# An encoder block on one core: one ring of raw weight tiles through the last gate/up block and the first down group, and its forms reloaded later and closer together

## The chip, the core and the metric

The kernel runs on one core of one Trainium2 chip. The metric is the device time of a whole execution in microseconds (us), taken as the median of three runs. TensorE (PE), VectorE (DVE), ScalarE (ACT), GpSimd (POOL) and SyncE (SP) each work through a queue of their own in order; SP, ACT and POOL also issue DMAs.

## What is computed

One encoder layer in fp32 on 512 tokens of width 2048: a norm, an input projection, two attention mixers, an output projection, and then the part in which the change lies, SwiGLU with D_FF = 5632, and a last norm.

```python
h2 = rmsnorm(x, g_ffn[layer])
gate, up = jnp.split(jnp.einsum('bsd,df->bsf', h2, w_gate_up[layer]), 2, axis=-1)
x = x + jnp.einsum('bsf,fd->bsd', jax.nn.silu(gate) * up, w_down[layer])
return rmsnorm(x, g_final)
```

## The kernel before

Every fp32 product is made of split numbers: a high half rounded to fp32r and a low half, the rest, and three matmuls (high by high, high by low, low by high; lines 227 to 229). The SwiGLU products are done in blocks of columns by a scheme with seven forms, m1 to m7: each form is a product of sums of quarter matrices, which saves one product in eight and needs sums of weights.

**Blocks and units.** Gate and up take eleven blocks, f0 = 0, 4, ..., 40 (block 40 is the last). A block runs the chain m1, m7, m6, m2, m5, m4, m3 with eight units each, 56 units; a unit is six matmuls. Down takes three groups of 6, 8 and 8 pairs (`DOWN_PAIRS`), two column blocks a group: the two blocks of six pairs (d6) have 42 units, the four of eight pairs (d8) 56.

**Weights.** Two units share one split of 128x1024 weights. It is made from raw tiles of 512 KB, loaded on SP's queue (line 272; 28 a gate/up block, 12 a d6 block), some combined first on VectorE (line 972). ScalarE makes the high half (line 836), VectorE the low half (line 839), into a ring of four `wide` pairs. All raws of one tag form a ring: a load is written into the program, a few units ahead of its use (up to 20 us by the kernel's own count), as soon as fewer than `RAWS[tag]` tiles are alive. Blocks 0 to 36 use twelve (`craw`), whose tiles are handed on by a list (`kept_raws`, for the tags in `KEPT_TAGS`); the last block has a ring of ten of its own (`craw40`), the d6 blocks another ten (`draw6`), the d8 blocks fifteen (`draw8`).

**Results of gate/up.** Snapshots of forms (`s1`, `s7`, `s6`) and their sums turn into silu(gate) * up. This is transposed by DMA (SP, line 1257), put together on ScalarE (line 1263), the sums of quarter matrices for the down product are made on VectorE (line 378), and all seven forms of a pair go to DRAM from the tile `pair` by a POOL DMA (`store`, line 1266). Two such stores belong to a block; in the last block the second comes 55 units after the last unit of m3, in the second d6 block.

**Forms of a down group.** They are read back, form by form, into the `arena` where the old forms have been used (`next_forms`). Of a group of six pairs a form comes in two parts, four pairs (512 KB) and two pairs (256 KB), into two `fr` tiles in turn: load on ScalarE's DMA queue (line 1306), high half on ScalarE (line 1309), low half on VectorE (line 1312). `turn` is the unit of the high half; the load is hooked five units ahead of it and the low half two units behind, and turns lie at least four units apart. The turns of the first group, counted from the first unit of the last gate/up block, are m1 8 and 12, m7 20 and 24, m6 32 and 36, m2 44 and 48, m5 56 and 60, m4 68 and 72, m3 80 and 84. The last block's snapshots are `slot` tiles; a down block's evictions (`ev`, line 1333) go to six more, which POOL adds to DRAM (`x1d`, line 1334).

All is written out by hand: at each unit the loop issues loads and splits that are due, the unit's matmuls, and the hooked steps; each engine's queue keeps that order.

Of the kernel before, what the change touches and what calls it, by code (L numbers as in the profile page):

```python
# [11 lines left out]
F32 = mybir.dt.float32  # L12
# [8 lines left out]
P = 128  # L21
# [4 lines left out]
KD = D // P  # L26
# [23 lines left out]
SPILLED = {"A": 4, "B": 6}  # L50
TWINS = 8
WIDE = 4
WIDE_AHEAD = 9.5
RAWS = {"raw": 6, "craw": 12, "craw1": 24, "craw0": 24, "kraw": 9, "craw40": 10, "draw6": 10, "draw8": 15}
KEPT_TAGS = ("craw",)
W_TILES = {"wi": 10, "wo": 12}
DOWN_PAIRS = (6, 8, 8)
ORDER = ("m1", "m7", "m6", "m2", "m4", "m5", "m3")
# [1 line left out]
EVICT = 6  # L60
# [15 lines left out]
def encoder_block(ctx, tc, x, w_in, g_q_a, g_k_a, w_out, w_gate_up, w_down, g_final, x_t, gains, c_ident, c_mask,  # L76
# [15 lines left out]
    def slot(base, dtype=F32, shape=(P, 512)):  # L92
        return sp.tile(list(shape), dtype, tag="s", name=nm(base))
# [25 lines left out]
    stage = wp.tile([P, 20, 512], F32, tag="stage", bufs=1, name="stage")  # L119
    homes = deque(stage[:, n] for n in range(8, 20))  # L120
    homing = [True]
    kept_raws = deque()
    extra_homes, retired = {}, []

    def more_homes(name, tile):
# [189 lines left out]
    def hook(n, f):  # L315
        hooks.setdefault(n, []).append(f)
# [886 lines left out]
    def hold(name, shape, dtype=F32):  # L1203
        if name not in held:
            held[name] = sp.tile([P] + list(shape), dtype, tag=name, bufs=1, name=nm(name))
        return held[name]

    forms_dram = dp.tile([P, 7, NFF // 2, 256], F32, tag="forms", name="forms")
    def gate_up_block(f0):
# [1 line left out]
        st = {}  # L1211

        def tile2(name):
            st[name] = [slot(name) if f0 == 40 else hold(f"{name}{t}", [512]) for t in range(2)]
            return st[name]

        def snap(form, name):
# [60 lines left out]
        for n, late in enumerate((3, 4, 6, 7)):  # L1278
            box.after("m3", late, lambda n=n: planes(("glo", "uhi")[n // 2], n // 2, n % 2))
            box.after("m3", late + 7, lambda n=n: turn(n))  # L1280
        for j, late in enumerate((23, 50 if f0 == 40 else 36)):
            for n, part in enumerate(((1, 0, 4, 1024), (0, 2, 4, 0), (0, 0, 2, 256))):
                box.after("m3", late + n, lambda j=j, part=part: merge(j, *part))
            box.after("m3", late + 3, lambda: pair_sums(hpart[0]))
            box.after("m3", late + 5, lambda j=j: store(f0 // 2 + j))
        return box

    for f in range(0, NFF, 4):
        box = gate_up_block(f)

    def load_x1(c, rows):
        for t in rows:
# [3 lines left out]
    def next_forms(box, first, pairs):  # L1296
        seq, turns = sorted(CHAIN, key=box.at.get), [0]

        def ready(form, h):
            m, st = ORDER.index(form), {}  # L1300
            lo_q, n = 4 * h, min(4, pairs - 4 * h)
            hi, lo = (form_tile(m, slice(lo_q, lo_q + n))[:, :, j] for j in range(2))

            def load():
                st["t"] = in_turn(frs, 2, [P, 4, 256], F32, "fr")[:, :n]
                nc.scalar.dma_start(st["t"], forms_dram[:, m, first + lo_q:first + lo_q + n])

            def split_hi():
                nc.scalar.activation(hi, st["t"], AF.Copy)

            def split_lo():
                nc.vector.tensor_tensor(lo, st["t"], f32(hi), op=OP.subtract)
            turn = max(box.at[form] + 4 * seq.index(form) + 4 * h + 1, turns[-1] + 4)
            turns.append(turn)
            hook(turn - 5, load)
            hook(turn, split_hi)
            hook(turn + 2, split_lo)
        for form in seq:
            for h in range(-(-pairs // 4)):
                ready(form, h)  # L1320
# [3 lines left out]
    def down_block(first, pairs, cb, last):  # L1324
# [3 lines left out]
        def add(form, i, j):  # L1328
            def go():
                for t in range(2):  # L1330
                    row = 2 * i + t
                    e = in_turn(evs, EVICT, [P, 512], F32, "ev")
                    nc.scalar.activation(e, box.bank_of(form)[t], AF.Copy, scale=r2["r"][:, row:row + 1])  # L1333
                    nc.gpsimd.dma_start(x1_dram[2 * cb + j, row], e, accum_op=OP.add)  # L1334
                if form in LAST_OF_BANK:
                    box.done(form)
            box.after(form, 0, go)
# [129 lines left out]
    def load_raws(n):  # L1467
        while done["load"] < len(units) and at[done["load"]] <= at[n] + units[done["load"]].load_ahead:
            for raw in units[done["load"]].raws:
                if raw.t is None:  # L1470
                    for r in live:
                        if last_use[r] < done["lo"] and r.homed and homing[0] and not any(r.t is h for h in retired):
                            homes.append(r.t)
                        elif last_use[r] < done["lo"] and not homing[0] and r.tag in KEPT_TAGS:
                            kept_raws.append(r.t)
                    live[:] = [r for r in live if last_use[r] >= done["lo"]]
                    if homing[0] and len(homes) <= (2 if xs[KD - 1] is None else 4 if done["load"] < 24 else 0):
                        return
                    if homing[0] and raw.tag == "raw" and sum(r.tag == "raw" for r in live) >= 2:
                        return  # L1480
                    if sum((r.tag == "raw") == (raw.tag == "raw") for r in live) >= RAWS[raw.tag]:
                        return
                    live.append(raw)
                    raw.load()
            done["load"] += 1
# [115 lines left out]
```

## Time and profile before

| | us |
|---|---|
| runs | 1962.06, 1963.46, 1964.12 |
| median | 1963.46 |
| the profiled execution | 1962.45 |
| its span in the profile | 1960.7 |
| TensorE busy | 1940.9 (99%) |
| VectorE busy | 1537.2 (78%) |
| ScalarE busy | 1129.3 (58%) |
| last gate/up block starts | 1444.2 |
| first and second d6 block start | 1526.2, 1583.4 |
| first d8 block starts | 1647.2 |

Busy times are those of the span. The profile is one execution; 1.75 us lie around its span. Line numbers are those of the kernel before. `PEclk` in the windows is the granted clock of TensorE, 1.00 for 2.4 GHz and 0.50 for 1.2 GHz; the DMA share is that of the core's sixteen DMA engines.

### The profile page before, as it was taken

The page shows a single profiled execution, that of the slowest core. Times are in us where ns is not written, and L with a number is a line of the kernel's source. Part 1 is how long each engine was busy: PE and PEld are TensorE (multiplying, and loading weights), DVE is VectorE, ACT ScalarE, POOL GpSimd, SP SyncE. Part 2 cuts the span into 40 slices and gives each one's busy share as a digit, 9 for nine tenths or more (in the row PEclk, how much of TensorE's full clock was granted, in tenths as well). Part 3 has the DMA queues.
Part 4 walks back from the last instruction along what each step waited for, and adds up shares of the span by engine and source line. Part 5 has one row for each costly group of instructions (what it writes and reads, how often), then busy time and mean ns, then how long its engine had stood idle before and what let it go on. Part 6 is the DMA issues. An engine that isn't in the chain of part 4 may idle for free.

```text
span 1960.7 us, 24582 instructions
## 1 busy us (share of the span) xinstructions
PE 1940.9 (99%) x8727; PEld 1600.7 (82%) x8727; DVE 1537.2 (78%) x2012; ACT 1129.3 (58%) x1649; POOL 140.2 (7%) x184
## 2 busy tenths in 40 slices
PE   9999999999999999999999999999999999999998
PEld 7888888888888888888888888888887887888886
DVE  7987778887775697778778778778787877787886
ACT  7655554565455565555555555555555656555555
POOL 1000011000000000000000000000000121111121
PEclk9999999999999999999999999999999999999999
DMA  9777693144342466858758757767678789868865
GB/s 345 236 258 236 210 280 108 59 145 156 102 151 97 172 209 188 295 150 274 262 151 284 242 173 278 224 197 283 200 231 288 202 220 296 225 157 252 225 146 167
DMA packets 256252, 410.35 MB, mean 209 GB/s; under 512 B 62912, under 2 KB 90048, under 8 KB 256000
## 3 DMA queue, kind: packets, MB, share of 16 engines
q1 hardware_dynamic: 225296, 322.17, 50.5%
q0 software_dynamic: 22480, 60.57, 12.4%
q10 hardware_dynamic: 8352, 26.05, 4.0%
q8 instruction: 68, 1.11, 0.2%
q14 instruction: 56, 0.46, 0.1%
HBM read 334.52 MB, written 62.65 MB: 203 GB/s over the span
## 4 chain that ended last, share of the span: by engine, by line
PE 91%; DVE 4%; issue 2%; DMA 2%; ACT 1%; POOL 0%; SPq 0%; DVEq 0%; POOLq 0%; ACTq 0%
PE b L229 29%; PE b L228 29%; PE b L227 29%; PE b L612 1%; DMA raw<-in_w_gate_up_dram 1%; DVE wide L839 1%; POOL x1d L1334 0%; PE b L1170 0%; DVE raw L972 0%; PE b L562 0%; DMA forms<-pair 0%; DMA raw<-in_w_in_dram 0%; DVE x L1124 0%; DMA raw<-in_w_down_dram 0%; DVE w L305 0%
## 5 line engine op out<-in xcount | busy, mean ns | idle before, releaser
L836 ACT ACTIVATE wide<-raw 128x1024 fp32r<-128x1024 f32 x462 | 487.2, 1059 | 474.3 <-PE b L229 265.7
L228 PE MATMUL b<-wide,arena 128*128 128x512 f32 x1848 | 721.4, 390 | 4.4 <-DVE wide L839 4.4
L227 PE MATMUL b<-wide,arena 128*128 128x512 f32 x1848 | 721.2, 390 | 3.1 <-ACT wide L836 2.5
L839 DVE TENSOR_TENSOR wide<-raw,wide 128x1024 fp32r<-128x1024 f32 x462 | 562.5, 1223 | 205.2 <-ACT wide L836 195.7
L229 PE MATMUL b<-wide,arena 128*128 128x512 f32 x1848 | 721.0, 390 | 0.0
L228 PEld LDWEIGHTS b<-wide,arena 128*128 128x128 f32 x1848 | 347.9, 188 | 77.8 <-DVE wide L839 5.6
L227 PEld LDWEIGHTS b<-wide,arena 128*128 128x128 f32 x1848 | 348.0, 188 | 76.0 <-ACT wide L836 2.9
L229 PEld LDWEIGHTS b<-wide,arena 128*128 128x128 f32 x1848 | 348.0, 188 | 72.6
L972 DVE TENSOR_TENSOR raw<-raw,raw 128x1024 f32<-128x1024 f32 x264 | 321.5, 1220 | 11.9 <-DMA raw<-in_w_gate_up_dram 11.8
L228 PE MATMUL b<-tw,arena 128*128 128x512 f32 x396 | 154.3, 390 | 0.6 <-DVE tw L895 0.6
L229 PE MATMUL b<-tw,arena 128*128 128x512 f32 x396 | 154.2, 389 | 0.0
L227 PE MATMUL b<-tw,arena 128*128 128x512 f32 x396 | 154.1, 389 | 0.0
L892 ACT ACTIVATE tw<-stage 128x512 fp32r<-128x512 f32 x140 | 85.5, 628 | 69.4 <-DVE stage L972 45.0
L895 DVE TENSOR_TENSOR tw<-stage,tw 128x512 fp32r<-128x512 f32 x140 | 93.9, 688 | 22.0 <-ACT tw L892 21.2
L218 ACT ACTIVATE pTh<-b 128x512 fp32r<-128x512 f32 x64 | 38.2, 597 | 101.0 <-PE b L612 95.7
L227 PE MATMUL b<-w,arena 128*128 128x512 f32 x240 | 95.8, 399 | 0.0
L229 PE MATMUL b<-w,arena 128*128 128x512 f32 x240 | 93.9, 391 | 0.0
L228 PE MATMUL b<-w,arena 128*128 128x512 f32 x240 | 93.5, 390 | 0.0
L1334 POOL DMA_DIRECT2D x1d<-ev x76 | 66.0, 962 | 318.0 <-ACT ev L1333 295.3
L378 DVE TENSOR_TENSOR pair<-pair 128x256 f32<-128x256 f32 x120 | 46.6, 422 | 53.6 <-ACT pair L1263 29.4
L228 PEld LDWEIGHTS b<-tw,arena 128*128 128x128 f32 x396 | 74.3, 188 | 16.8 <-DVE tw L895 1.5
L229 PEld LDWEIGHTS b<-tw,arena 128*128 128x128 f32 x396 | 74.3, 188 | 15.8 <-DVE arena L346 0.4
(229 smaller groups left out, 2107.0 us busy)
## 6 DMA issues: line engine op xcount, KB each, us to landing
raw<-in_w_gate_up_dram SPq DMA_DIRECT2D x308, 512.0 KB, 6.1
raw<-in_w_down_dram SPq DMA_DIRECT2D x88, 512.0 KB, 6.9
stage<-in_w_in_dram SPq DMA_DIRECT2D x111, 256.0 KB, 5.3
forms<-pair POOLq DMA_DIRECT2D x22, 896.0 KB, 8.2
x1d<-ev POOLq DMA_DIRECT2D x76, 256.0 KB, 6.2
fr<-forms ACTq DMA_DIRECT2D x35, 512.0 KB, 6.2
raw<-in_w_out_dram SPq DMA_DIRECT2D x32, 512.0 KB, 4.2
stage<-in_w_in_dram SPq DMA_DIRECT2D x90, 128.0 KB, 3.4
```

Source lines behind the costliest of these rows:

```text
L218: nc.scalar.activation(hi, src, AF.Copy)
L227: nc.tensor.matmul(dst, ah, bh, start=start, stop=False, skip_group_check=chained)
L228: nc.tensor.matmul(dst, ah, bl, start=False, stop=False, skip_group_check=chained)
L229: nc.tensor.matmul(dst, al, bh, start=False, stop=stop, skip_group_check=chained)
L378: nc.vector.tensor_tensor(out, x, y, op=op)
L612: nc.tensor.transpose(ps[:, t * P:(t + 1) * P], self.p[t][:, kb * P:(kb + 1) * P], ident)
L836: nc.scalar.activation(self.hi, self.src, AF.Copy)
L839: nc.vector.tensor_tensor(self.lo, self.src, f32(self.hi), op=OP.subtract)
L892: nc.scalar.activation(self.pair[:, 0], self.src, AF.Copy)
L895: nc.vector.tensor_tensor(self.pair[:, 1], self.src, f32(self.pair[:, 0]), op=OP.subtract)
L972: nc.vector.tensor_tensor(t[dst], t[src[0]], t[src[1]], op=OP.add if form == "m6" else OP.subtract)
L1334: nc.gpsimd.dma_start(x1_dram[2 * cb + j, row], e, accum_op=OP.add)
```

## The change

- One ring of twelve raws goes on from block 36 through the last block and the d6 blocks: `craw40` and `draw6` are among the tags whose tiles are handed on. At unit 28 of the last block two of the twelve tiles leave the list (`DROP_AT`), and ten remain. `draw8` becomes 16.
- The last block's snapshots use the held tiles `s1`, `s6`, `s7`, as other blocks do, and the evictions of the down blocks use these six tiles in turn.
- The second store of the last block and what leads to it come ten units earlier (40 instead of 50 units after m3).
- The first group's forms are reloaded from unit 7 + 30 of the last block on in steps of three. The turns become m1 37 and 40, m7 43 and 46, m6 49 and 52, m2 55 and 58, m5 61 and 64, m4 67 and 70, m3 73 and 76. For all groups turns may lie three units apart; the load is four units ahead of the turn and the low half one behind.

```diff
+RELOAD_AT = 30
+RELOAD_STEP = 3
+DROP_AT = 28
-RAWS = {"raw": 6, "craw": 12, "craw1": 24, "craw0": 24, "kraw": 9, "craw40": 10, "draw6": 10, "draw8": 15}
-KEPT_TAGS = ("craw",)
+RAWS = {"raw": 6, "craw": 12, "craw1": 24, "craw0": 24, "kraw": 9, "craw40": 10, "draw6": 10, "draw8": 16}
+KEPT_TAGS = ("craw", "craw40", "draw6")
...
-            st[name] = [slot(name) if f0 == 40 else hold(f"{name}{t}", [512]) for t in range(2)]
+            st[name] = [hold(name, [2, 512])[:, t] for t in range(2)]
...
-        for j, late in enumerate((23, 50 if f0 == 40 else 36)):
+        for j, late in enumerate((23, 40 if f0 == 40 else 36)):
...
+    last_gate = box.at["m1"] - KD // 2 + 1
...
-            turn = max(box.at[form] + 4 * seq.index(form) + 4 * h + 1, turns[-1] + 4)
+            turn = max(box.at[form] + 4 * seq.index(form) + 4 * h + 1, turns[-1] + RELOAD_STEP)
+            if first == 0:
+                turn = max(box.at[form] + 1, box.at["m1"] + RELOAD_AT, turns[-1] + RELOAD_STEP)
             turns.append(turn)
-            hook(turn - 5, load)
+            hook(turn - RELOAD_STEP - 1, load)
             hook(turn, split_hi)
-            hook(turn + 2, split_lo)
+            hook(turn + RELOAD_STEP - 2, split_lo)
...
-                    e = in_turn(evs, EVICT, [P, 512], F32, "ev")
+                    if not evs:
+                        evs.extend(held[name][:, t] for name in ("s1", "s6", "s7") for t in range(2))
+                    evs.append(evs.pop(0))
+                    e = evs[-1]
...
                         elif last_use[r] < done["lo"] and not homing[0] and r.tag in KEPT_TAGS:
-                            kept_raws.append(r.t)
+                            if n >= last_gate + DROP_AT and dropped[0] < RAWS["craw"] - RAWS["draw6"]:
+                                dropped[0] += 1
+                            else:
+                                kept_raws.append(r.t)
...
-                    if sum((r.tag == "raw") == (raw.tag == "raw") for r in live) >= RAWS[raw.tag]:
+                    most = RAWS["craw"] if raw.tag == "craw40" and n < last_gate + DROP_AT else RAWS[raw.tag]
+                    if sum((r.tag == "raw") == (raw.tag == "raw") for r in live) >= most:
```

Three places in the queues show what this moves. On ScalarE, before, behind the silu of the last block's `s1` (`wide` are the splits, `fr` the tiles of the reloads, `pair` and `turned` the putting together of the results):

```order
L836 ACTIVATE wide_525_5840<-raw_556_10700 128x1024
L1263 ACTIVATE pair_467_5381<-turned_550_6452 128x1024
L1236 ACTIVATE s1_565_10828<-s1_565_10828,fixed_81 128x512
L1236 ACTIVATE s1_566_10829<-s1_566_10829,fixed_81 128x512
L836 ACTIVATE wide_527_5842<-raw_558_10720 128x1024
L1263 ACTIVATE pair_467_5381<-turned_550_6452 128x512
L1309 ACTIVATE arena5_85<-fr_562_10790 128x2x256
L1263 ACTIVATE pair_467_5381<-turned_550_6452 128x512
L836 ACTIVATE wide_529_5844<-raw_560_10738 128x1024
L1306 DMA fr_561_10789<-forms_138 128x1024
L836 ACTIVATE wide_531_5846<-raw_564_10820 128x1024
```

The same place in the changed program:

```order
L1266 ACTIVATE pair_467_5381<-turned_547_6449 128x1024
L1239 ACTIVATE s1_544_6071<-s1_544_6071,fixed_81 128x512 x2
L839 ACTIVATE wide_527_5842<-raw_521_5811 128x1024
L1266 ACTIVATE pair_467_5381<-turned_547_6449 128x512
L1311 DMA fr_549_11034<-forms_138 128x512
L1266 ACTIVATE pair_467_5381<-turned_547_6449 128x512
L1314 ACTIVATE arena2_84<-fr_548_11033 128x4x256
L839 ACTIVATE wide_529_5844<-raw_524_5838 128x1024
L1311 DMA fr_548_11033<-forms_138 128x1024
L839 ACTIVATE wide_531_5846<-raw_535_5906 128x1024
L1314 ACTIVATE arena2_84<-fr_549_11034 128x2x256
```

Before, one reload's high half and one load stand among four splits; now two loads and two high halves stand among three, and the reload in work is that of m1 where it was that of m6.

On POOL, the last of the stores of forms among the adding writes of the evictions, before:

```order
L1334 DMA x1d11_127<-ev_598_11376 128x512
L1334 DMA x1d20_130<-ev_599_11377 128x512
L1334 DMA x1d21_131<-ev_600_11378 128x512
L1334 DMA x1d32_136<-ev_601_11379 128x512
L1334 DMA x1d33_137<-ev_602_11380 128x512
L1266 DMA forms_138<-pair_467_5381 896x1x256
L1334 DMA x1d22_132<-ev_597_11375 128x512
```

And now:

```order
L1344 DMA x1d11_127<-s1_544_6071 128x512
L1269 DMA forms_138<-pair_467_5381 896x1x256
L1344 DMA x1d20_130<-s6_546_6203 128x512
L1344 DMA x1d21_131<-s6_546_6203 128x512
L1344 DMA x1d32_136<-s7_545_6137 128x512
L1344 DMA x1d33_137<-s7_545_6137 128x512
L1344 DMA x1d22_132<-s1_544_6071 128x512
```

The store is four adding writes further ahead.

On SP, the loads of the end of the second d6 block and the beginning of the first d8 block (`raw_615` and `raw_616` are the last two loads of the second d6 block, the waits named DMASW are on POOL's stores of forms), before:

```order
L272 DMA raw_614_11725<-in_w_down_dram 128x2x512 [waits DMAHW0_49,DVE_49]
L272 DMA raw_615_11848<-in_w_down_dram 128x2x512 [waits DMASW4_49,DMASW5_49,DMASW3_49,DMASW6_49,DMASW2_49,DMASW7_49,DMASW1_49,DMAHW1_49,DMASW0_49,DMAHW5_49,DVE_49,Activation_49]
L272 DMA raw_616_11870<-in_w_down_dram 128x2x512 [waits DMAHW6_49]
L272 DMA raw_617_11946<-in_w_down_dram 128x2x512 [waits DMAHW7_49]
L272 DMA raw_618_11964<-in_w_down_dram 128x2x512 [waits DMAHW0_49]
```

And now, where `raw_538` and `raw_535` are the last two of the d6 block and `raw_550` is the first of the d8 block:

```order
L275 DMA raw_538_5940<-in_w_down_dram 128x2x512 [waits DMAHW4_49,DVE_49]
L275 DMA raw_535_5906<-in_w_down_dram 128x2x512 [waits DMAHW6_49,DVE_49,Activation_49]
L275 DMA raw_550_11880<-in_w_down_dram 128x2x512 [waits DMASW5_49,DMASW4_49,DMASW6_49,DMASW3_49,DMASW7_49,DMASW2_49,DMAHW7_49,DMASW1_49,DMASW0_49]
L275 DMA raw_551_11897<-in_w_down_dram 128x2x512 [waits DMAHW0_49]
L275 DMA raw_552_11908<-in_w_down_dram 128x2x512 [waits DMAHW1_49]
```

The wait for the stores has moved from the eleventh load of the second d6 block to the first load of the d8 block.

## Rows read from the trace of the kernel before

**Rows 1.** The chain that ended last, by engine (section 4 of the page)
```profile
PE 91%; DVE 4%; issue 2%; DMA 2%; ACT 1%; POOL 0%; SPq 0%; DVEq 0%; POOLq 0%; ACTq 0%
```

**Rows 2.** Waits of TensorE, 1368 to 1960: waited for, us in total, times, longest
```profile
PE b L228 <- DVE wide L839: 4.4, 3, 3.5
PE b L227 <- ACT wide L836: 2.5, 1, 2.5
```

**Rows 3.** Windows, block by block: blocks 36 and 40, both d6, first d8
```profile
core 0: us, PE busy (x) PEld busy (x) DVE busy (x) ACT busy (x) POOL busy (x), PEclk, DMA share, GB/s
1368.10:1444.20 76.10, 76.10 (x337) 63.04 (x336) 60.12 (x63) 43.02 (x48) 1.82 (x2) 1.00 0.68 218
1444.20:1526.20 82.00, 78.36 (x337) 64.06 (x336) 67.99 (x72) 48.97 (x56) 1.81 (x2) 0.98 0.82 260
1526.20:1583.40 57.20, 57.20 (x254) 47.27 (x253) 47.15 (x47) 39.66 (x47) 7.96 (x9) 1.00 0.80 212
1583.40:1647.20 63.80, 60.58 (x254) 49.33 (x253) 45.95 (x44) 38.83 (x46) 16.45 (x19) 0.95 0.92 247
1647.20:1723.30 76.10, 76.10 (x337) 63.05 (x336) 61.60 (x54) 44.89 (x50) 12.13 (x14) 1.00 0.87 235
```

**Rows 4.** Chain pieces before the first stop: start us, us, what
```profile
1482.61 6.55 DMA raw<-in_w_gate_up_dram
1489.18 1.24 DVE raw L972
```

**Rows 5.** Timeline around it: start us, us, instruction, idle before and releaser
```profile
1490.32 1.22 DVE L839 TENSOR_TENSOR wide<-raw,wide 128x1024 fp32r<-128x1024 f32 x1
1491.59 0.50 PE L228 MATMUL b<-wide,arena 128*128 128x512 f32 x1 [3.46 <-DVE wide L839]
```

**Rows 6.** Chain pieces around the second stop
```profile
1609.32 5.97 DMA forms<-pair
1615.54 4.61 DMA raw<-in_w_down_dram
1620.23 1.06 ACT wide L836
1621.32 1.24 DVE wide L839
1622.60 0.79 PE b L228
1623.39 0.43 PE b L229
...
1629.42 0.23 PE b L229
```

**Rows 7.** Waits of the SP queue, 1444 to 1660
```profile
SPq L272 <- DMA forms<-pair: 37.5, 1, 37.5
```

**Rows 8.** Windows: the busiest stretch, and the stretches behind the two stops
```profile
1494.60:1526.20 31.60, 31.42 (x136) 25.68 (x135) 29.96 (x34) 20.14 (x23) 0.91 (x1) 0.98 1.01 366
...
1492.30:1495.70 3.40, 3.40 (x10) 2.63 (x9) 3.37 (x4) 1.35 (x2) 0.00 (x0) 0.50 0.99 357
1622.00:1628.80 6.80, 6.20 (x15) 4.85 (x16) 5.20 (x6) 5.39 (x7) 1.72 (x2) 0.50 1.06 357
```

**Rows 9.** VectorE's low halves of reloads, and the window, 1494.6 to 1547
```profile
L1312 DVE TENSOR_TENSOR arena<-fr,arena 128x1024 fp32r<-128x1024 f32 x4 | 4.9, 1222 | 0.0
...
L1312 DVE TENSOR_TENSOR arena<-fr,arena 128x512 fp32r<-128x512 f32 x3 | 2.1, 687 | 0.0
1494.60:1547.00 52.40, 52.22 (x228) 42.92 (x227) 50.36 (x54) 37.02 (x42) 4.47 (x5) 0.99 0.89 275
```

**Rows 10.** ScalarE's high halves of the large reloads, 1494.6 to 1547
```profile
L1309 ACT ACTIVATE arena<-fr 128x1024 fp32r<-128x1024 f32 x4 | 4.2, 1050 | 1.0 <-DMA fr<-forms 1.0
```

**Rows 11.** Issues 1494 to 1583; landings of fr 1526 to 1600, then 1440 to 1600
```profile
fr<-forms ACTq DMA_DIRECT2D x4, 512.0 KB, 8.1
DMA to landing us min/median/max: 3.9/6.6/8.5
DMA to landing us min/median/max: 2.7/6.3/8.5
```

**Rows 12.** Timeline of VectorE and of TensorE at the next block's start
```profile
1519.64 1.23 DVE L839 TENSOR_TENSOR wide<-raw,wide 128x1024 fp32r<-128x1024 f32 x1
1526.21 0.39 PE L227 MATMUL b<-wide,arena 128*128 128x512 f32 x1
```

More of the change, by code (lines that the diff above doesn't have):

```diff
@@ L121, in encoder_block @@
     homing = [True]
-    kept_raws = deque()
+    kept_raws, dropped = deque(), [0]
     extra_homes, retired = {}, []
```

## The prediction

> **What bounds the kernel now.** I read four views in this order: the shares of the chain, the waits of TensorE, its blocks one by one, and the two places where it stops. The chain that ended last is 91% TensorE [rows 1], and from block 36 to the last down block TensorE waits only for splits of weights: 4.4 us in three waits on VectorE's low half and 2.5 us in one wait on ScalarE's high half [rows 2]. So nothing but those stops, and what they do to the clock, can be won in the region of the change. Block by block [rows 3]: block 36, 56 units, takes 76.1 us with PE busy for all of it (1.36 us a unit); the last gate/up block takes 82.0 us for the same 336 matmuls, 5.9 more; the first down block (42 units) takes 57.2, the second 63.8, 6.6 more. The first block of eight pairs is back at 76.1. The two excesses, 12.5 us, are all that there is to take.
>
> Stop A: in the last gate block a raw leaves SP's queue at 1482.61, lands 6.55 us later, and the combination that needs it starts at 1489.18 [rows 4]. TensorE has by then stood for 3.46 us, to 1491.59 [rows 5]. Stop B: the first load of the second down block's tail is released by the landing of the last forms store (issued 1609.32, 5.97 us), lands 4.61 us after its own issue, and goes through both splits to the matmul at 1622.60 [rows 6]; SP stood for 37.5 us on that one store [rows 7]. After both stops the granted clock is 0.50, the 1.2 GHz level, for 3.4 and 6.8 us [rows 8], and the matmuls there follow at 0.43 us instead of 0.23 [rows 6]: eight and sixteen of them, some 1.6 and 3.2 us of the 5.9 and 6.6.
>
> **The ring.** The last gate block keeps twelve raws, as block 36 has, until its unit 28, and inherits them from the ring instead of starting ten of its own. Block 36 with twelve has no stop at all [rows 3], and the stop at unit 32 (43.5 us, or 32 units, into the block) is the effect of a raw that could leave only when a tile of ten was read. I take the whole of stop A off: -5.9. Bounds: -5.9 and -3 (if the drop to ten brings half of it back at a later unit). Nothing is added: as many loads, combinations and splits as before. The snapshots and evictions write into other tiles, at the same number and size: 0. The larger ring of the eight-pair blocks serves blocks that lose nothing already: 0.
>
> **The store.** The loads of both six-pair blocks are now ahead of every wait on the forms stores in SP's queue; the wait stands on the first load of the first eight-pair block. The store itself comes ten units earlier, 13.6 us, so it lands near 1601.7 on the old time line (1615.3 less 13.6), while that block begins at 1647.2: a load of 4.6 us and both splits (1.06 and 1.24, [rows 6]) fit in well. Behind the store on POOL now stand four adding writes that were ahead of it; nothing on TensorE's path reads them. -6.6, bounds -6.6 and -3.4 (if a shorter wait stays, without the half clock's 3.2).
>
> **The reloads.** This is where the change can cost. Fourteen reloads of forms (seven of 512 KB, seven of 256 KB) lay between units 8 and 84, counted from the start of the last gate block; now they lie between 37 and 76. Each is one DMA on ScalarE's queue, one ScalarE high half and one VectorE low half.
>
> *VectorE's time.* In 1494.6 to 1547.0, which holds nearly the new stretch, VectorE was busy for 50.36 of 52.4 us, with seven low halves in it, 4.9 and 2.1 us [rows 9]. All fourteen take 7 x 1.22 + 7 x 0.69 = 13.4, so 6.4 more, 56.8. But after stop A it was also making up its lead: the split that starts at 1519.64 ends 5.3 us before the block that uses it begins at 1526.21 [rows 12], and at 1491.6 that lead was nothing [rows 5]. Without stop A it need not earn these 5.3: 51.5 of 52.4. It just fits, with no room to catch up; I book 0 to 2 us, and 0.7.
>
> *The turn of a tile.* There are two tiles, one for the large and one for the small reloads, in turn. With three units between reloads a tile comes round every six units, 8.16 us. In that time its load has to land, ScalarE has to read it (1.05 us [rows 10]), VectorE too (1.22 [rows 9]), and only then can ScalarE issue the next load. ScalarE works in order: while it waits for a landing or for the tile, every split behind it waits as well, then VectorE's, then TensorE. The large ones landed in 8.1 us (median of four) between 1494 and 1583, over all reloads there in 6.6, and the whole region goes from 2.7 to 8.5 with 6.3 as the middle [rows 11]. Four large turns fall into the gate block, whose raws keep the DMA engines busy; there I take 8.1, the row nearest to it: 4 x (8.1 + 1.05 + 1.22 - 8.16) = 8.8 us. Three fall into the first down block, which moves less: with 6.6, 3 x (6.6 + 2.27 - 8.16) = 2.1 us. The delay of 10.9 us first eats the lead of 5.3 and then shows on TensorE: 5.6, with VectorE's 0.7 6.3 us. Bounds: with 6.3 throughout the delay is 7 x 0.41 = 2.9, less than the lead, so 0; with 8.5 throughout it is 7 x 2.61 = 18.3 less 5.3, so 13. The load's lead at the first turn is four units, 5.4 us, and before it was five.
>
> *The later reloads* keep their turns, with the load a unit later: up to 8.5 - 5.4 = 3.1 us of waiting on ScalarE for one of them, under the 5.3 of lead. 0, bounds 0 and 2.
>
> **The sum.** Against the profiled run of 1962.45 us (span 1960.7 and 1.75 around it), 1.0 under the median of the three runs, 1963.46: -5.9 - 6.6 + 6.3 = -6.2. On the median: 1957.3 us. The new stops are of 1 to 2 us each at units 55 to 76, and I book no half clock for them: the rows have one after 3.46 us of standing and one after two waits in a row [rows 5, 6, 8], longer than these.
>
> **Rivals.**
> *Hidden reloads (1951).* If a reload takes turns with the raws at the DMA engines instead of waiting behind them, it has half of the 366 GB/s that moved in the busiest stretch [rows 8]: 512 KB in 2.9 us, and with the 2.0 us that the quickest landing (2.7 us, 256 KB, of which 0.7 is moving) leaves as a fixed part, 4.9 us. A turn is then 4.9 + 2.27 = 7.2, under 8.16, and all 12.5 us stay won. For it: the low end of the landings, and a DMA stream that no longer has to make up stop A. Against it: the median of 8.1 [rows 11]. The Trainium skill has this as a rule: DMA: Bandwidth & Descriptors, section Queues, rings and completion order, says that each DMA engine goes round the queues that have work, a packet at a time. The 8.1 us speak against a full half share here. Chance 0.25.
>
> *All given back (1962).* The landings stay at 8.1 in the down block as well, since the first loads of the second down block and the eight-pair block come earlier and fill the gap: 7 x 2.21 = 15.5, less 5.3, plus 0.7 is 10.9, so -1.6. With a raw of the first down block also late by up to 2 us it is no change at all, 1962 to 1964. For it: VectorE at 96% [rows 9]. Chance 0.28, for 1959.5 to 1967.4.
>
> *Slower (1970).* The same 10.9 us, but the stops come close enough together that the clock falls to 1.2 GHz after them. Priced by the two stretches of before, 1.6 and 3.2 us each; three of them at 2.4 are 7.2, so -12.5 + 10.9 + 7.2 = +5.6, 1969. This decides as soon as stops add more than 16.4 us. Against it: it needs the slowest landings and the clock together. Chance 0.10.
>
> *The store's wait stays.* Should the d6 loads still be held by a store, stop B remains and the sum is +0.4: 1963.9. The order of SP's queue speaks against it; it is within the 0.28.
>
> **How the numbers follow.** The forecast, 1953 to 1959.5, has 0.37, the hidden reloads 0.25, all given back 0.28, slower 0.10. A measurement of this kernel tells 0.2% (3.9 us) from no change. Faster is then 0.62, same 0.28, slower 0.10. The range of 1950.5 to 1964.0 takes in the full gain and most of the third case, and leaves out some 0.05 below, 0.05 between and 0.10 above.
>
> **What would show it.** The last gate block at 76 to 80 us with no wait of over 2 us at its unit 32; the second down block at 57.2 to 59, with SP's wait on the store on an eight-pair load. ScalarE waiting for reloads (the group of high halves from the reload tile) for 8 to 12 us in all, and TensorE's new waits between the gate block's last ten units and the first twenty of the down block, with 5 to 7 us. If the landings there are under 6 us, TensorE stands for nothing and the time is 1951. If VectorE is late with the reloads landed, the term of its time was too small. If a wait of TensorE stands elsewhere, the ring of ten in the down blocks is what I have missed.

## The result and the profile after

| | before | after |
|---|---|---|
| median of six runs, us | 1962.86 | 1971.20 |
| lowest to highest | 1961.54 to 1964.12 | 1967.88 to 1973.72 |
| the profiled execution | 1962.45 | 1973.72 |
| its span | 1960.7 | 1972.0 |

The ratio is 1.0041, with a 95% interval of 1.0028 to 1.0054: the changed kernel is slower by 0.4%. The profiled execution is the slowest of its six, so its stops are read for where they are, and sizes are taken from the medians of runs where that can be done.

The windows of the changed kernel, block by block, as [rows 3] (last gate/up block, the two d6 blocks, the first three d8 blocks; line numbers in rows of the changed kernel and of the runs made from it are their own):

```profile
core 0: us, PE busy (x) PEld busy (x) DVE busy (x) ACT busy (x) POOL busy (x), PEclk, DMA share, GB/s
1445.60:1522.30 76.70, 76.46 (x337) 62.85 (x336) 61.01 (x65) 43.67 (x50) 1.81 (x2) 1.00 0.75 239
1522.30:1589.90 67.60, 61.03 (x254) 47.86 (x253) 54.16 (x55) 45.32 (x55) 10.60 (x12) 0.97 0.79 210
1589.90:1653.50 63.60, 59.32 (x254) 48.32 (x252) 46.46 (x43) 36.39 (x43) 13.86 (x16) 0.97 0.97 268
1653.50:1733.00 79.50, 77.84 (x338) 62.64 (x337) 62.31 (x55) 45.72 (x51) 12.13 (x14) 1.00 0.80 206
1733.00:1809.40 76.40, 76.35 (x338) 62.96 (x336) 55.99 (x48) 42.77 (x49) 12.14 (x14) 1.00 0.77 205
1809.40:1886.90 77.50, 76.55 (x337) 63.18 (x338) 62.24 (x55) 45.80 (x51) 12.17 (x14) 1.00 0.84 219
```

An undisturbed block takes 76.16 us (56 units) or 57.15 (42). The last gate block has 0.5 us left of its 5.9: stop A is gone. But the first d6 block, which lost nothing before, loses 10.4, the second still loses 6.5, and the d8 blocks 3.3, 0.2 and 1.3 us. That is 22 us, where before it was 12.5; the difference is 9.7 of the 11.3 us between the two profiled executions. The rest lies ahead of block 40, which started 1.3 us later (1445.56 and 1444.23) though the two programs do the same work up to there; this is not explained here.

TensorE's waits from block 36 on, as [rows 2] (waited for: us in total, times, longest):

```profile
PE b L231 <- DVE wide L842: 9.7, 9, 3.6
PE b L230 <- ACT s L1343: 3.6, 2, 2.8
```

The second row is new: TensorE waits for ScalarE's eviction of a finished bank (line 1343), which no row of before shows.

Pieces of the chain of waits (start us, us, what) and rows of the timeline (start us, us, instruction, idle before and releaser) show what ended last. In the last gate block, the tile of the large reloads:

```profile
1502.99 7.66 DMA fr<-forms
1510.68 1.07 ACT arena L1314
1511.77 1.24 DVE arena L1317
1513.03 7.01 DMA fr<-forms
```

Landing, high half, low half, the next load: 1502.99 to 1513.03 is one turn of 10.0 us, for the 8.16 that six units give. The end of the first d6 block's reloads, first in the chain, then on ScalarE:

```profile
1549.59 6.94 DMA fr<-forms
...
1557.61 0.58 ACT s L1343
...
1559.52 0.43 PE b L230
```

```profile
1554.57 1.06 ACT L839 ACTIVATE wide<-raw 128x1024 fp32r<-128x1024 f32 x1 [1.96 <-DVE raw L975]
1556.56 1.06 ACT L1314 ACTIVATE arena<-fr 128x1024 fp32r<-128x1024 f32 x1 [0.92 <-DMA fr<-forms]
```

A reload is issued at 1549.59 and lands 6.94 us later. Behind its high half on ScalarE stand the evictions, and TensorE's next form needs the bank that they empty. ScalarE stands only 0.92 us for the landing itself; it comes late to it, since the split before had waited 1.96 us for VectorE's combination. TensorE stood for 2.8 us, and the matmuls that follow start 0.43 us apart, the 1.2 GHz level, about nine of them. In the whole block TensorE waits 3.6 us for evictions and 2.8 for splits, 6.4 of the 10.4; the nine slow matmuls are some 1.8 more.

The second d6 block: the eleventh of its loads in the chain, and then what stands behind it on ScalarE, VectorE and TensorE:

```profile
1613.39 10.21 DMA raw<-in_w_down_dram
```

```profile
1623.68 1.06 ACT L839 ACTIVATE wide<-raw 128x1024 fp32r<-128x1024 f32 x1 [5.86 <-DMA raw<-in_w_down_dram]
1624.64 1.04 ACT L1314 ACTIVATE arena<-fr 128x1024 fp32r<-128x1024 f32 x1
1625.72 1.23 DVE L1317 TENSOR_TENSOR arena<-fr,arena 128x1024 fp32r<-128x1024 f32 x1 [6.64 <-ACT arena L1314]
1626.86 1.22 DVE L975 TENSOR_TENSOR raw<-raw,raw 128x1024 f32<-128x1024 f32 x1
1628.00 2.51 DVE L842 TENSOR_TENSOR wide<-raw,wide 128x1024 fp32r<-128x1024 f32 x2
1629.27 0.49 PE L231 MATMUL b<-wide,arena 128*128 128x512 f32 x1 [3.62 <-DVE wide L842]
```

The ring of ten has a place for the eleventh load only at 1613.39, 23.5 us into the block, and it lands 10.21 us later. ScalarE's split stands 5.86 us for it, and the high half of a reload stands behind that split. VectorE has the low half of this reload next in its queue and stands for it for 6.64 us; the combination of the next raws (line 975) and the splits that TensorE needs come only after it. TensorE stands for 3.6 us at unit 26, where stop B was, and goes on at the lower clock. The store has no part in it, nor has the landing of this reload, which was issued at 1612.38 and took 6.8 us: it lay ready for over 4 us. So it is the order of two in-order queues that ends last here. SP's wait of this stretch, 1590 to 1660, and ScalarE's waits for reloads of the first group, 1480 to 1580:

```profile
SPq L275 <- DVE wide L842: 47.9, 8, 29.2
```

```profile
ACT arena L1314 <- DMA fr<-forms: 9.0, 3, 4.1
```

### The profile page after: what moved, and what is told of

Its sections match the earlier page's. It is cut to its first block, busy times and chain, and to the rows that moved or that the text cites. A ratio compares the mean times of both kernels' runs of the same rounds, so it can differ in the third digit from the quotient of the medians.

```text
span 1972.0 us, 24578 instructions
## 1 busy us (share of the span) xinstructions
PE 1945.6 (99%) x8727; PEld 1600.8 (81%) x8727; DVE 1538.6 (78%) x2012; ACT 1127.3 (57%) x1649; POOL 140.2 (7%) x184
## 4 chain that ended last, share of the span: by engine, by line
PE 85%; DVE 6%; DMA 5%; ACT 2%; issue 2%; ACTq 0%; DVEq 0%; POOLq 0%; POOL 0%; SPq 0%
PE b L231 27%; PE b L232 27%; PE b L230 27%; DMA fr<-forms 4%; PE b L615 1%; DVE raw L975 1%; DVE wide L842 1%; ACT wide L839 1%; ACT arena L1314 1%; DMA raw<-in_w_down_dram 1%; DVE arena L1317 1%; PE b L1173 0%; PE b L565 0%; ACT pair L1266 0%; DVE x L1127 0%
## 5 line engine op out<-in xcount | busy, mean ns | idle before, releaser
L898 DVE TENSOR_TENSOR tw<-stage,tw 128x512 fp32r<-128x512 f32 x140 | 93.8, 687 | 23.5 <-ACT tw L895 22.7
L1344 POOL DMA_DIRECT2D x1d<-s x76 | 66.0, 980 | 330.9 <-ACT s L1343 311.8
L231 PEld LDWEIGHTS b<-tw,arena 128*128 128x128 f32 x396 | 74.4, 188 | 16.8 <-DVE tw L898 1.5
L230 PEld LDWEIGHTS b<-tw,arena 128*128 128x128 f32 x396 | 74.4, 188 | 15.6
L232 PEld LDWEIGHTS b<-tw,arena 128*128 128x128 f32 x396 | 74.4, 188 | 15.2
```

Of the source, the lines that this page charges most:

```text
L230: nc.tensor.matmul(dst, ah, bh, start=start, stop=False, skip_group_check=chained)
L231: nc.tensor.matmul(dst, ah, bl, start=False, stop=False, skip_group_check=chained)
L232: nc.tensor.matmul(dst, al, bh, start=False, stop=stop, skip_group_check=chained)
L898: nc.vector.tensor_tensor(self.pair[:, 1], self.src, f32(self.pair[:, 0]), op=OP.subtract)
```

## Experiments

All ratios are to runs of the kernel before on the same chip, with 95% intervals. "Loss" is a block's window over 76.16 or 57.15 us.

### x1_store: the kernel before, the second store ten units earlier

```diff
-        for j, late in enumerate((23, 50 if f0 == 40 else 36)):
+        for j, late in enumerate((23, 40 if f0 == 40 else 36)):
```

> The kernel before with the last block's second store ten units earlier and nothing else. If the wait for the store was all of stop B, the second down block of six pairs takes 57 to 58 us instead of 63.8 and the median is 1956 to 1957. If the ring of ten holds the eleventh load of that block anyway (its tile comes free near unit 17, 12 us ahead of the use at unit 26, and a landing took 4.6 to 12 us), the stop shrinks to 0 to 3 us with or without the half clock: 1957 to 1961. Stop A stays at 5.8 us by both.

Measured: 1957.89 us, ratio 0.9977 (0.9968 to 0.9986). Its windows (last gate block, both d6 blocks):

```profile
1446.10:1528.20 82.10, 78.43 (x337) 64.05 (x336) 67.92 (x72) 49.12 (x56) 1.82 (x2) 0.98 0.85 257
1528.20:1585.30 57.10, 57.10 (x253) 47.30 (x252) 46.30 (x47) 40.43 (x48) 10.47 (x12) 1.00 0.83 218
1585.30:1642.40 57.10, 57.10 (x253) 47.29 (x252) 46.30 (x43) 37.73 (x45) 13.98 (x17) 1.00 0.98 271
```

Stop B is gone to the last tenth, as the first theory has it, though the median lies in the second one's range; stop A is as it was. SP still waits for the store in the second d6 block, but for 23.7 us instead of 37.5 [rows 7]:

```profile
SPq L272 <- DMA forms<-pair: 23.7, 1, 23.7
```

So that wait costs nothing once it ends well before the load is used, and the store's term of the sum stands by the trace. The medians moved by 4.7 us, less than the block's 6.6; the profiled execution's block 40 started 1.9 us later than that of before, which is not explained here.

### x2_later_old: the changed kernel, later groups reloaded as before

```diff
-            turn = max(box.at[form] + 4 * seq.index(form) + 4 * h + 1, turns[-1] + RELOAD_STEP)
             if first == 0:
                 turn = max(box.at[form] + 1, box.at["m1"] + RELOAD_AT, turns[-1] + RELOAD_STEP)
+            else:
+                turn = max(box.at[form] + 4 * seq.index(form) + 4 * h + 1, turns[-1] + 4)
             turns.append(turn)
-            hook(turn - RELOAD_STEP - 1, load)
+            lead, behind = (RELOAD_STEP + 1, RELOAD_STEP - 2) if first == 0 else (5, 2)
+            hook(turn - lead, load)
             hook(turn, split_hi)
-            hook(turn + RELOAD_STEP - 2, split_lo)
+            hook(turn + behind, split_lo)
```

> The changed kernel with the forms of the second and third group reloaded as before (steps of four, load five units ahead, low half two behind); the first group's stay in steps of three. If the shorter lead is what stops TensorE from the second d6 block on, that block takes 57 to 59 us instead of 63.6, the first and third d8 block 76.2 instead of 79.5 and 77.5, and the median is near 1960. If the second d6 block stops because of its ring or as a late effect of the first group, it still takes 62 to 64 and the median is 1964 to 1967. The first d6 block keeps its 10 us of loss by both.

Measured: 1960.25 us, ratio 0.9988 (0.9979 to 0.9998). Both d6 blocks:

```profile
1522.70:1590.20 67.50, 61.03 (x253) 47.81 (x252) 53.95 (x54) 45.22 (x55) 10.60 (x12) 0.97 0.82 212
1590.20:1648.20 58.00, 57.45 (x253) 47.18 (x253) 46.57 (x44) 37.70 (x45) 13.84 (x16) 1.00 0.98 268
```

The first d6 block loses its 10.4 us as in the changed kernel, the second only 0.9, and the first d8 block takes 76.2 again. The median falls by 11 us. So the stops from the second d6 block on are made by the later groups' reloads; they are neither the ring's doing alone nor a late effect of the first group. The eleventh load of the second d6 block leaves at 1613.55 here, 23.3 us into the block against 23.5 in the changed kernel, and the block loses only 0.9 us: that the ring holds this load is not by itself the stop.

### x3_step4: the changed kernel, all reloads in steps of four

```diff
-RELOAD_STEP = 3
+RELOAD_STEP = 4
```

> The changed kernel with steps of four instead of three for all reloads (so the first group's turns are 37, 41, ..., 89, a tile comes round every eight units, 10.9 us, the load is five units ahead and the low half two behind). Theory of the tile's turn: landing and both halves of 8 to 10.4 us fit into 10.9, the first d6 block loses 0 to 2 us instead of 10.4, the d8 blocks nothing: 1951 to 1955, and 1957 to 1959 if the second d6 block keeps its stop for a cause of its own. Theory of VectorE's time: the reloads take as long as before on VectorE and end fifteen units later, so the first d6 block loses about half as much, 4 to 6 us: 1956 to 1961.

Measured: 1956.12 us, ratio 0.9966 (0.9953 to 0.9979). Last gate block and both d6:

```profile
1446.30:1522.50 76.20, 76.20 (x337) 62.96 (x336) 63.20 (x66) 44.47 (x51) 1.82 (x2) 1.00 0.74 240
1522.50:1582.70 60.20, 58.46 (x253) 46.84 (x252) 51.21 (x52) 43.98 (x53) 10.58 (x12) 1.00 0.85 231
1582.70:1640.80 58.10, 57.53 (x254) 47.20 (x254) 46.65 (x44) 37.76 (x45) 13.84 (x16) 1.00 1.00 272
```

One unit more between reloads (and with it one more of lead, and the low half one later) turns 15 us: no loss in the gate block, 3.1 in the first d6 block, 1.0 in the second, none in the first d8 block (76.1). It is faster than the kernel before. The median lies at the low end of the second theory's range, and the first d6 block's 3.1 us between the two (0 to 2, 4 to 6): of its 10.4 us 7.3 go with the step. ScalarE's waits for the first group's landings, 1480 to 1580, are no shorter than in the changed kernel:

```profile
ACT arena L1314 <- DMA fr<-forms: 8.8, 3, 3.7
```

So what the longer step gives is room to catch up behind them.

### x4_noload: twelve of the first group's loads left out

```diff
-                nc.scalar.dma_start(st["t"], forms_dram[:, m, first + lo_q:first + lo_q + n])
+                if first or form == "m1":
+                    nc.scalar.dma_start(st["t"], forms_dram[:, m, first + lo_q:first + lo_q + n])
```

> The changed kernel with twelve of the first group's fourteen loads left out (only the forms of m1 are loaded; the other high and low halves are made from what then lies in the tiles, so the output is not the reference's). ScalarE's and VectorE's work and order stay. Theory of the landings: the first d6 block loses 0 to 2 us instead of 10.4, the rest as in the changed kernel: 1959 to 1963 (under 1957 if the later stops were its late effect). Theory of VectorE's time: the block still loses 6 to 10 us: 1966 to 1971.

Measured: 1963.60 us, ratio 1.0004 (0.9995 to 1.0013), a little above the range. Both d6 blocks and the first d8 block:

```profile
1521.80:1580.70 58.90, 57.45 (x254) 47.25 (x253) 49.35 (x50) 40.99 (x50) 10.28 (x12) 1.00 0.69 173
1580.70:1643.80 63.10, 59.29 (x254) 48.29 (x253) 46.45 (x43) 36.38 (x43) 14.19 (x17) 0.97 0.97 271
1643.80:1721.90 78.10, 77.11 (x338) 62.81 (x337) 62.41 (x55) 45.56 (x51) 12.13 (x14) 1.00 0.82 213
```

With the halves still made in steps of three and no landings to wait for, the first d6 block loses 1.8 us. So 8.6 of its 10.4 go with the twelve loads: their landings, and whatever their traffic does to the raws beside them, which this run takes away too (173 GB/s in the block instead of 210). The 1.8 left are VectorE's and ScalarE's own time; 1.4 of them are one wait for an eviction. The later blocks keep 6.0 and 1.9 us, with the first group on time: again, these stops are not its late effect.

### y1_lead4 and y2_space3: the later groups' hooks and their spacing apart

Both have the first group in steps of four as x3_step4, and for the others

```diff
             if first == 0:
+                turn = max(box.at[form] + 1, box.at["m1"] + 30, turns[-1] + 4)
+            else:
+                turn = max(box.at[form] + 4 * seq.index(form) + 4 * h + 1, turns[-1] + 4)
...
+            lead, behind = (4 + 1, 4 - 2) if first == 0 else (4, 1)
```

in y1_lead4, and in y2_space3

```diff
+                turn = max(box.at[form] + 4 * seq.index(form) + 4 * h + 1, turns[-1] + 3)
...
+            lead, behind = (4 + 1, 4 - 2) if first == 0 else (5, 2)
```

> The changed kernel with the first group in steps of four (as in the run with steps of four, 1956), and the later groups with turns four apart but the changed hooks: load four units ahead, low half one behind. If the shorter lead alone makes ScalarE stand for landings and so the eleventh load of the second d6 block late, that block takes 62 to 64 us and the d8 blocks lose 2 to 5: 1962 to 1967. If it is the spacing of three, nothing is lost there: 1956.

> The complement: first group in steps of four, later groups with the hooks of before (load five ahead, low half two behind) but turns that may lie three apart. If the spacing makes the stops of the second d6 block and of the d8 blocks: 1962 to 1967; if the lead does: 1956 to 1957.

Measured: y1_lead4 1960.94 us, 0.9988 (0.9979 to 0.9997); y2_space3 1955.07 us, 0.9961 (0.9946 to 0.9976). The second d6 block and the first and third d8 block of y1_lead4:

```profile
1583.40:1642.80 59.40, 57.76 (x254) 47.15 (x253) 46.32 (x43) 36.76 (x43) 13.84 (x16) 1.00 0.99 275
1642.80:1721.70 78.90, 77.11 (x338) 62.86 (x337) 62.22 (x55) 45.66 (x51) 12.14 (x14) 1.00 0.83 221
1797.80:1875.10 77.30, 76.46 (x337) 63.00 (x336) 61.84 (x55) 45.67 (x51) 12.18 (x14) 1.00 0.84 221
```

The second d6 and the first d8 block of y2_space3:

```profile
1581.10:1638.60 57.50, 57.50 (x254) 47.25 (x254) 46.43 (x44) 37.52 (x45) 14.07 (x17) 1.00 0.99 270
1638.60:1714.70 76.10, 76.10 (x337) 63.06 (x336) 61.59 (x54) 44.57 (x50) 12.13 (x14) 1.00 0.88 239
```

ScalarE's waits for the later groups' 28 reloads, 1583 to 1900, first of y1_lead4, then of y2_space3:

```profile
ACT arena L1314 <- DMA fr<-forms: 22.2, 13, 4.6
```

```profile
ACT arena L1314 <- DMA fr<-forms: 3.7, 4, 1.3
```

The spacing alone costs nothing (y2_space3 is a little under its range). The hooks alone cost 2.3, 2.7 and 1.1 us in the three blocks and 4.8 us of median over x3_step4, 4.5 if each is set against the kernel before on its own chip: less than the 6 to 11 expected, but the whole sign. The hooks are two edits, the load a unit later and the low half a unit earlier, and no run parts them. In the trace the load's part shows: with its lead of four units, 5.4 us, ScalarE stands for 13 of the 28 reloads, 22.2 us in all, and with five units for 4, 3.7 us.

The eleventh load of the second d6 block leaves y2_space3 at 1604.45, 23.3 us into the block, and ScalarE stands for it as long as in the changed kernel:

```profile
1608.88 1.22 DVE L975 TENSOR_TENSOR raw<-raw,raw 128x1024 f32<-128x1024 f32 x1
1613.57 1.06 ACT L839 ACTIVATE wide<-raw 128x1024 fp32r<-128x1024 f32 x1 [6.08 <-DMA raw<-in_w_down_dram]
1614.66 1.23 DVE L842 TENSOR_TENSOR wide<-raw,wide 128x1024 fp32r<-128x1024 f32 x1 [4.56 <-ACT wide L839]
```

But here VectorE has made the next combination before it stands, no low half of a reload is in between, and TensorE does not stop.

### z1_first4: only the first group in steps of four

The later groups are those of the changed kernel: turns three apart and a lead of four.

```diff
             if first == 0:
+                turn = max(box.at[form] + 1, box.at["m1"] + 30, turns[-1] + 4)
+            else:
+                turn = max(box.at[form] + 4 * seq.index(form) + 4 * h + 1, turns[-1] + 3)
...
+            lead, behind = (4 + 1, 4 - 2) if first == 0 else (4, 1)
```

> The changed kernel with only the first group's steps and hooks set to four (load five ahead, low half two behind); the later groups stay as in the changed kernel (turns three apart, load four ahead, low half one behind). Theory that the second d6 block's stop of 6.4 us is made by the later groups alone: it stays, with 2 to 5 us in the d8 blocks, 1964 to 1967. Theory that it needs the delay of the first group too: that block loses 1 to 3 us as with the lead of four alone, 1960 to 1962.

Measured: 1965.24 us, ratio 1.0010 (1.0001 to 1.0019), as the first theory has it. Both d6 blocks:

```profile
1521.40:1583.60 62.20, 59.30 (x254) 46.60 (x253) 51.78 (x53) 44.10 (x53) 10.58 (x12) 1.00 0.84 226
1583.60:1646.10 62.50, 59.39 (x254) 48.31 (x253) 46.39 (x43) 36.52 (x43) 13.87 (x16) 0.97 0.99 275
```

The second d6 block loses 5.4 us and the first d8 block 2.2 with the first group in steps of four. So these stops are made by the later groups, and the one in the d6 block takes both of their edits: the spacing alone gives 0.4 us there, the hooks alone 2.3, the two together 5.4, with the fall of the clock in them (0.97 in the window). The queues show why: VectorE stands 5.72 us for a reload's high half with the next combination behind it, as in the changed kernel (6.64) and in x4_noload (6.03). In y1_lead4 and y2_space3, with one of the edits each, that combination stands ahead of the reload's low half. How much the first group's late end adds to the 6.5 of the changed kernel, some 1 us, is within what two profiled executions can differ by: the first d6 block loses 5.1 us here and 3.1 in x3_step4, with the same steps.

The medians make one sum: from x3_step4 (1956.1) the first group's step of three costs 4.1 us (x2_later_old), the later groups' two edits 9.1 (z1_first4; 8.6 if each is set against the kernel before on its own chip), together 1969.3; the changed kernel has 1971.2.

### y3_ring10: ten raws handed on from the start of the last gate block

Reloads as before the change (turns, steps of four and hooks), store at 40. The two tiles leave the list from eight units ahead of the block.

```diff
-DROP_AT = 28
+DROP_AT = -8
...
+            turn = max(box.at[form] + 4 * seq.index(form) + 4 * h + 1, turns[-1] + 4)
...
+            hook(turn - 5, load)
...
+            hook(turn + 2, split_lo)
```

> The store ten units earlier and the raws handed on from block 36 as in the changed kernel, but with ten tiles from the start of the last gate block instead of twelve until unit 28; reloads as before the change. Beside the run with the store alone (1957.9, ten tiles of its own, stop A of 5.9 us). If stop A comes from having ten raws alive, it stays: the last gate block takes 81 to 83 us and the median is 1957 to 1959. If it comes from starting a new ring of tiles, the block takes 76 to 78 and the median is 1952 to 1954.

Measured: 1964.01 us, ratio 1.0005 (0.9996 to 1.0015), outside both ranges. Last gate block:

```profile
1444.10:1532.40 88.30, 80.41 (x337) 65.03 (x336) 67.94 (x72) 49.01 (x56) 1.82 (x2) 0.96 0.75 236
```

The gate block loses 12.1 us, twice as much as with ten tiles of its own; the d6 blocks take 57.2 and 59.1 us. So it isn't the new ring that makes stop A: with ten tiles handed on it comes as well. With twelve until unit 28 it doesn't (0.5 us in the changed kernel, 0.0 in x3_step4), but in those runs the reloads have been put off too. Why handing on ten is worse than ten new ones was not tried.

Twelve raws together with the early reloads of before were not run; by the sizes in the program the two reload tiles and the two extra raws want 8 KB a partition each, and the change has the extra raws leave before the reload tiles come. Ten raws together with the late reloads, which would take the two causes apart, were not run either.

### y4_at28 and z2_at28_space3: two units earlier

```diff
-RELOAD_AT = 30
-RELOAD_STEP = 3
+RELOAD_AT = 28
+RELOAD_STEP = 4
```

This is y4_at28. z2_at28_space3 has the same 28 and 4 written into the first group's lines, and the later groups of y2_space3.

> The changed kernel with steps of four and the first turn two units earlier (35, 39, ..., 87). In the run with steps of four the first d6 block lost 3.1 us, in its units 5 to 33, where reloads and splits met. If the loss is what is left of reloads that end too late, two units earlier give 1 to 2 us back: 1954 to 1955.5. If it is VectorE's time, nothing changes (1956), and if the earlier loads meet the raws behind the drop to ten tiles, the last gate block loses 1 to 3 us: 1957 to 1959.

> First group in steps of four from two units earlier on (as in the run at 1955.2), later groups with turns three apart and the hooks of before (as in the run at 1955.1). If the two small gains over the run with steps of four (1956.1) are real and add up: 1953.5 to 1954.5; if they are scatter: 1955 to 1956. Either way faster than the kernel before by 0.3 to 0.5%.

Measured: y4_at28 1955.24 us, 0.9962 (0.9947 to 0.9976); z2_at28_space3 1953.88 us, 0.9951 (0.9937 to 0.9964), the fastest here. In y4_at28 the gate block takes 77.3 us and the first d6 block 58.2. Last gate block and both d6 blocks of z2_at28_space3:

```profile
1445.80:1523.50 77.70, 76.92 (x337) 62.83 (x336) 64.14 (x67) 46.38 (x53) 1.82 (x2) 1.00 0.76 237
1523.50:1582.40 58.90, 57.86 (x254) 47.18 (x253) 50.63 (x52) 42.95 (x52) 10.45 (x12) 1.00 0.88 228
1582.40:1639.50 57.10, 57.10 (x254) 47.22 (x253) 46.35 (x44) 37.46 (x45) 14.01 (x17) 1.00 1.02 279
```

The two units move 1.1 to 1.5 us of loss into the gate block and take 1.3 to 2.0 out of the first d6 block. Against x3_step4 the intervals overlap, so which of these three (or of four, with y2_space3) is best stays open; that they all beat the kernel before by 0.3 to 0.5% does not.

## Why the prediction was wrong, point by point

**The ring: its size right, its cause read and not shown.** -5.9 was booked, the gate block kept 0.5 us, and the drop to ten at unit 28 brought no stop back. That the two raws alone do this no run shows: wherever there are twelve, the first group's reloads have left the first half of the block too. For the raws speaks a row of the kernel before. Just ahead of the combination that frees the tile of [rows 4], VectorE was idle for ScalarE's putting together of the results, so no low half of a reload held it up there:

```profile
1480.22 1.22 DVE L378 TENSOR_TENSOR pair<-pair 128x256 f32<-128x256 f32 x3 [2.07 <-ACT pair L1263]
```

**The store: right, but its place was taken.** x1_store has the 6.6 us alone. In the changed kernel a stop stands at the same unit 26 for another cause. In [rows 7] SP waits 37.5 us for the store, and that wait hid that the ring holds the same load nearly as long: SP's 29.2 us in the changed kernel. "Fit in well" was said of the d8 block's first load; the eleventh load of the d6 block, which the prediction had declared free, was not priced against the ring. By itself this hold is cheap: in x2_later_old and y2_space3 the load leaves as late, and the block loses 0.9 and 0.4 us.

**The first group: the right place, and both of its sizes off.** Booked were 6.3 us, with the stops between the gate block's last ten units and the first twenty of the d6 block. There they were, 0.5 and 10.4. The signs named for it held: ScalarE stood 9.0 us for these reloads (8 to 12 named), TensorE 6.6 in all (5 to 7 named). The landings were shorter than the 8.1 and 6.6 of the sum, over the group

```profile
DMA to landing us min/median/max: 2.6/5.8/7.7
```

and yet the loss was larger. The step that failed is "the delay first eats the lead of 5.3 and then shows". That lead belongs to the splits, and their waits are 3.0 of the 6.6 us. ScalarE's queue also holds the evictions, and there TensorE waits for a bank at the moment it has finished it, with no lead at all: 3.6 us in two waits, the longer one followed by the half clock, for which nothing was booked. VectorE's 0.7 us was 1.8 with ScalarE's own time (x4_noload), within its bounds.

**The later groups: the term that decided.** "0, bounds 0 and 2" was 11 us by the medians of the changed kernel and x2_later_old. A single wait of up to 3.1 us was held against the lead of 5.3, as if each wait stood alone and the lead were whole again before the next. With a lead of 5.4 us ScalarE stands for 13 of the 28 reloads (y1_lead4), and the lead isn't earned back; that is the smaller part, 4.8 us. For the rest, which comes when the turns lie closer as well, the prediction had no term: it priced landings, and not where a reload's halves stand in the queues. No reload landed late there. A low half came to stand ahead of the combination of the next raws, and waited 6.64 us for a high half that stood behind a split without its raw. Runs show which two edits it takes together; that it is this order is read from the traces, and no run moves the low half alone.

**The rivals.** "Slower (1970)" named the time but not the way: it put three falls of the clock behind the first group's landings of 8.1 us. There were two falls, one behind an eviction and one behind the splits of unit 26, and half of the loss lay in reloads that it didn't name. Its 16.4 us of new stops were exceeded with 22. "Hidden reloads" is refuted for steps of three. Its estimate for a large reload that takes turns with the raws was 4.9 us; the two in the gate block took 7.66 and 7.01 in the chain above. So a reload has less than half of the engines there: while the first of them was on its way, three queues moved data, and the reload's packets took 18.5% of the engines' time, SP's 61.3% and POOL's 24.6%. That the DMA engines go round the queues that have work is a rule of the Trainium skill (DMA: Bandwidth & Descriptors, Queues, rings and completion order); no run here takes it apart. "All given back" had 10.9 us for the first group, just what the two blocks lost, but by luck: it had landings of 8.1 us throughout, and neither evictions nor a fall of the clock. The chance of 0.62 for faster rested on the 0 for the later groups.

## What to carry to other kernels

An in-order queue that waits for a transfer holds back everything behind it, and each of these has its own slack: a split made ahead has some, an eviction of the bank that is needed next has none. A prefetch distance shortened by a unit is priced against the slowest landings, and for all the transfers together. Where an edit moves an instruction past another in such a queue, ask what it will wait for there and who then stands behind it. Where a change bundles a gain with a tighter schedule, undo the schedule alone: here one constant was worth 15 us, and one line of the change (the earlier store) over a third of what was to be had.

## What the runs showed of the hardware

In the changed kernel a 512 KB reload landed in 3.4 us where little else moved (issued at 1531.38) and in 7.0 and 7.7 us beside SP's raws in the gate block. But those issued at 1549.59 and 1597.36 took 6.9 and 6.8 us without raws, the last 0.8 us of the first apart: there POOL's queue, with the adding writes, had 50.4% and 40.5% of the engines' time. So the same distance was enough in one place and too short in another. The raw loads of a burst in the second d6 block of the changed kernel took 10.2 and 8.2 us, then 10.2 and, one after the other, up to 12.8 for the sixth. After its two longest stops, 2.8 and 3.6 us, the granted clock was at the 1.2 GHz level for about nine and eight matmuls; after waits of up to 1.2 us in the same blocks the matmuls went on at 0.23 us.
